# Fourteen row tiles in seven block products, outputs accumulated on PSUM banks that ScalarE copies, token sums in the residual's buffer, and a new order in each group

## The chip, the cores and the metric

The kernel runs on one core of a Trainium2 chip. The metric is the device time of one execution in microseconds (us); the time of the kernel before is the median of three runs, and one further execution was profiled. The engines are TensorE (PE in the profile, PEld for its weight loads), VectorE (DVE), ScalarE (ACT), GpSimd (POOL) and SyncE (SP). Here SP and POOL mainly issue DMAs.

## The reference

One encoder layer on 256 tokens of width 2048, in float32. Most of its work is matrix products:

```python
def _swiglu(u, w_gate, w_up, w_down):
    return (jax.nn.silu(u @ w_gate) * (u @ w_up)) @ w_down
...
        f = _swiglu(_rmsnorm(h, ffn1_pre_g[i]), ffn1_w_gate[i], ffn1_w_up[i], ffn1_w_down[i])
        h = h + 0.5 * _rmsnorm(f, ffn1_post_g[i])
        m = _mixer(_rmsnorm(h, mix_pre_g[i]), w_qkv[i], na_rpb[i], out_g[i], w_o[i])
        h = h + _rmsnorm(m, mix_post_g[i])
        f = _swiglu(_rmsnorm(h, ffn2_pre_g[i]), ffn2_w_gate[i], ffn2_w_up[i], ffn2_w_down[i])
        h = h + 0.5 * _rmsnorm(f, ffn2_post_g[i])
        g = jax.nn.sigmoid(_rmsnorm(h, ple_pre_g[i]) @ w_ple_gate[i])
        h = h + _rmsnorm(g * (p[i] @ w_ple_proj[i]), ple_post_g[i])
```

The hidden width of both feed-forward blocks (FFN1, FFN2) is 5632. The mixer is attention with 16 heads; the last part is a small gated product (PLE).

## The kernel before

**Precision.** A float32 operand is split into a high and a low part (`_h`, `_l`; weights `wh`, `wl`), and a product takes three matmuls for each row tile and token tile: high by high (L104), low by high (L105), high by low (L106), all in `mac`. The tokens are the stationary operand (128x128), the weights stream past (128x512). A row tile is 128 of the 2048 input rows, so there are 16; a token tile is 128 of the 256 tokens, so there are two. `split` (L71) makes the two parts of two row tiles of weights at once: a cast on ACT (L77), a subtraction on DVE (L78), in six buffers each that go round in turn.

**Groups.** Each FFN walks over the hidden width in eleven groups (`nb` 0 to 10) of 512 columns. A group has four outputs, gate and up for two token tiles: g0, g1, u0, u1, each one PSUM bank. Then comes SiLU(gate) times up, eight transposes to `hid` (`tr`), and, within the next group, four "down" blocks of 24 matmuls, which bring the hidden columns of the group before to the width of 2048 and are added to `f` by DVE (L436). `fill()` takes the next waiting down block at fixed places of the group.

**Block products.** Groups 1 to 10 don't compute all outputs by the plain product. `ROWS` (L29) pairs six row tiles with six others. With tokens as a 2x2 block matrix (token tile by half of the rows) and weights likewise (half of the rows by gate or up), `pair_product` (L164) uses the Strassen-Winograd form, seven block products for eight. Three of them have plain tokens (u) as stationary operand: a11, a12 and a22. Four have sums of tokens (`sums_h`, `sums_l`): s1 to s4, made once for each FFN by `token_sums` (L300). The weights of the products are sums too: `add_rows` (L193) adds the up weights to gate weights in place by POOL DMAs that accumulate, and `add` does further ones on DVE (L204). The four row tiles that are left ("rest") are multiplied plainly for all four outputs. The outputs are put together from the products: `kept` (L173) copies a product from PSUM to SBUF on ACT (L175), and DVE adds or subtracts (L206).

**Order.** The engines run their instructions in the order of the program, which a scheduler draws up from the order of the code. A buffer's next writer waits for its last reader. The order in a group before is a11, s4, the transposes of the group before, half of the rest for u, a down block, s1, the other half, down, s2, down, s3, a12, a22, down, the rest for g. Weight loads are issued on SP in this order too, each waiting there until its buffer is free.

```python
        ra1, rb2 = blocks(wa, 0, ca), blocks(wb, 1, cb)
        g1 = bank("g1")
        mac(g1, a11, split_rows(ra1), first=True, last=True)
        g0_ = kept("g0_s", g1)
```

**Around the FFNs.** `h`, the residual, stays in SBUF all the time. `load_h` (L369) loads it in FFN1's group 0, where `prenorm_factor` (L376) squares it. `residual` (L384) adds an FFN's result to it at the end.

Of the kernel before, what the change touches and what calls it, by code (L numbers as in the profile page):

```python
# [15 lines left out]
P = 128  # L16
D = 2048
# [11 lines left out]
ROWS = (0, 1, 2, 3, 8, 9), (4, 5, 6, 7, 10, 11)  # L29
# [5 lines left out]
def encoder_layer(ctx: ExitStack, tc: tile.TileContext, a: dict, out: bass.AP):  # L35
# [35 lines left out]
    def split(raw):  # L71

        n, m = raw.shape[1:]
        wh = wpool.tile([P, 2, NB], F32R, name="wh", bufs=6)[:, :, :m]
        wl = wpool.tile([P, 2, NB], F32R, name="wl", bufs=6)[:, :, :m]
        splits[:] = [
            nc.scalar.copy(wh[:, :n], raw),  # L77
            nc.vector.tensor_tensor(wl[:, :n], raw, wh[:, :n].bitcast(F32), op=ALU.subtract),  # L78
        ]
        return [(wh[:, i], wl[:, i]) for i in range(n)]  # L80
# [83 lines left out]
    def pair_product(lhs, sums, wa, ca, wb, cb, fill, rest_first):  # L164

        rows1, rows2 = ([lhs[k] for k in ks] for ks in ROWS)
        a11, a12, a22 = of_tile(rows1, 0), of_tile(rows2, 0), of_tile(rows2, 1)
        s1, s2, s3, s4 = sums
# [4 lines left out]
        def kept(name, x):  # L173
            t = ffn_pool[0].tile([P, NB], F32, name=name, tag="part", bufs=3)
            nc.scalar.copy(t, x)  # L175
            return t

        def spans(j, step):
            for k0, k1 in ((0, KB), (KB, RQ)):
                for k in range(k0, k1, step):  # L180
                    yield k, min(k + step, k1)
# [5 lines left out]
        def blocks(w, j, c):  # L187
            raw = ffn_pool[0].tile([P, RQ, NB], F32, name="raw_b", bufs=3)
            for k0, k1 in spans(j, KB):
# [3 lines left out]
        def add_rows(raw, w, j, c):  # L193
            for k0, k1 in spans(j, 2):
                nc.gpsimd.dma_start(raw[:, k0:k1], weight_rows(w, j, c, k0, k1), accum_op=ALU.add)  # L195

        def split_rows(raw):
            return sum((split(raw[:, k : min(k + 2, RQ)]) for k in range(0, RQ, 2)), [])

        def add(out_, x, y, op=ALU.add):  # L200
            n = x.shape[1] if len(x.shape) > 2 else 0
            for k in range(0, n, 2):
                j = slice(k, min(k + 2, n))
                nc.vector.tensor_tensor(out_[:, j], x[:, j], y[:, j], op=op)  # L204
            if not n:
                nc.vector.tensor_tensor(out_, x, y, op=op)  # L206

        nk = len(lhs)
        k_rest = [(k, (nk - 2 * RQ) // 2) for k in range(2 * RQ, nk, (nk - 2 * RQ) // 2)]

        def rest(w, k, n, c, accs_, last=False):
            parts = load_parts(w, k * P, n, c)
            for t, acc, lead in accs_:
                mac(acc, of_tile(lhs[k : k + n], t), parts, first=lead, last=last)

        def rest_b(i, last):
            rest(wb, *k_rest[i], cb, [(1, u1, i == 0), (0, u0, i == 0 and rest_first)], last=last)

        u0 = u1 = None
        if rest_first:  # L220
            u0, u1 = bank("u0"), bank("u1")
            rest_b(0, False)
            run_later()
        ra1, rb2 = blocks(wa, 0, ca), blocks(wb, 1, cb)
        g1 = bank("g1")
        mac(g1, a11, split_rows(ra1), first=True, last=True)
        g0_ = kept("g0_s", g1)
        add_rows(ra1, wb, 0, cb)
        u0 = u0 or bank("u0")
        mac(u0, s4, split_rows(rb2), first=not rest_first)  # L230
# [7 lines left out]
        u1_ = kept("u1_s", g0)
        add(ra1, ra1, rb2)
        add_rows(rb2, wb, 0, cb)  # L240
        if not rest_first:
            rest_b(1, True)
        fill()
        mac(g1, s2, split_rows(ra1), last=True)
        u0_ = kept("u0_s", g1)
        add(u0_, u0_, u1_, ALU.subtract)
        ra2 = blocks(wa, 1, ca)
        fill()
        mac(g1, s3, split_rows(rb2), last=True)
        add(u0_, u0, u0_, ALU.subtract)  # L250
        add(u1_, u1_, g1, ALU.subtract)
        add(u1_, u1, u1_)
        mac(g0, a12, split_rows(ra2), first=True)
        add(ra1, ra1, ra2)
        mac(g1, a22, split_rows(ra1))
        fill()
        for k, n in k_rest:
            rest(wa, k, n, ca, [(0, g0, False), (1, g1, False)], last=k + n == nk)
        assert len(k_rest) == 2
        add(g0_, g0, g0_)  # L260
        return (g0_, g1), (u0_, u1_)
# [38 lines left out]
    def token_sums(*parts):  # L300
# [3 lines left out]
        hi, lo = (  # L304
            sums_pool[0].tile([P, 2, 2, n_all, P], F32R, name=f"sums_{x}", tag=f"sums_{x}", bufs=1) for x in "hl"
        )
# [28 lines left out]
    h = resid.tile([P, NT, D], F32, name="h")  # L335
# [13 lines left out]
    def load_x(k):  # L349
# [7 lines left out]
        else:  # L357
            xb = ffn_pool[0].tile([P, 2, S], F32, name="xb", tag="gs", bufs=2)
# [25 lines left out]
    def residual(fg, ssf, scale, blocks, rs, g, sums=None, y_pool=None):  # L384
# [4 lines left out]
        r, y0 = [], []  # L389
        for b0 in range(0, D // NB, 2):  # L390
# [469 lines left out]
```

## Time and profile before

| | |
|---|---|
| time, median of three runs | 1928.42 us (1928.11 to 1928.62) |
| the profiled execution | 1928.43 us, of which its span from first to last instruction is 1926.7 us |
| mean granted clock of TensorE | 0.998 |
| FFN1's groups 1 to 10 and its end, 56.15 to 702.2 us | PE busy 645.43 of 646.05 us |
| attention and its output, 702.2 to 1109.1 us | PE busy 404.13 of 406.90 us |
| FFN2 up to its last groups, 1109.1 to 1742 us | PE busy 632.52 of 632.90 us |
| FFN2's end and PLE, 1742 to 1926.7 us | PE busy 171.26 of 184.70 us |

Rows of a timeline give start, duration, engine, line, operation, output<-inputs and shapes, and in brackets the engine's idle time before it and what ended that. Rows of groups give a count, busy time and mean duration in ns of one, then the idle time before them. A matmul's recorded duration overlaps the next one's; starts tell the pitch.

### The profile page before, as it was taken

The page shows a single profiled execution, that of the slowest core. Times are in us where ns is not written, and L with a number is a line of the kernel's source. Part 1 is how long each engine was busy: PE and PEld are TensorE (multiplying, and loading weights), DVE is VectorE, ACT ScalarE, POOL GpSimd, SP SyncE. Part 2 cuts the span into 40 slices and gives each one's busy share as a digit, 9 for nine tenths or more (in the row PEclk, how much of TensorE's full clock was granted, in tenths as well). Part 3 has the DMA queues.
Part 4 walks back from the last instruction along what each step waited for, and adds up shares of the span by engine and source line. Part 5 has one row for each costly group of instructions (what it writes and reads, how often), then busy time and mean ns, then how long its engine had stood idle before and what let it go on. Part 6 is the DMA issues. An engine that isn't in the chain of part 4 may idle for free.

```text
span 1926.7 us, 23362 instructions
## 1 busy us (share of the span) xinstructions
PE 1902.8 (99%) x8600; PEld 1562.8 (81%) x8600; DVE 1554.7 (81%) x1740; ACT 1128.8 (59%) x1364; POOL 172.4 (9%) x151
## 2 busy tenths in 40 slices
PE   8999999999999999999999999999999999999997
PEld 6888888888888878888888888888888888888786
DVE  7888898889898986666565588888988898889864
ACT  7666565666566554554545466665656655665653
POOL 0111101100110000000000010110011011100100
PEclk9999999999999999999999999999999999999999
DMA  9897778877887647454455568887778777875463
GB/s 350 241 251 232 232 203 228 240 229 223 214 246 234 170 157 247 143 175 155 151 179 182 186 210 238 224 239 233 210 210 248 225 228 212 245 224 162 160 226 114
DMA packets 207363, 408.41 MB, mean 212 GB/s; under 512 B 8849, under 2 KB 11921, under 8 KB 206737
## 3 DMA queue, kind: packets, MB, share of 16 engines
q1 hardware_dynamic: 174608, 344.00, 51.4%
q0 software_dynamic: 32640, 62.92, 18.8%
q8 instruction: 67, 1.10, 0.2%
q14 instruction: 48, 0.39, 0.1%
HBM read 404.79 MB, written 2.10 MB: 211 GB/s over the span
## 4 chain that ended last, share of the span: by engine, by line
PE 95%; DVE 2%; ACT 1%; issue 1%; DMA 1%; POOL 0%; SPq 0%; DVEq 0%; POOLq 0%; ACTq 0%
PE pair_g L105 10%; PE pair_g L104 10%; PE pair_g L106 10%; PE down L105 8%; PE down L104 8%; PE down L106 8%; PE pair_u L104 3%; PE pair_u L105 3%; PE pair_u L106 3%; PE v L106 2%; PE v L105 2%; PE v L104 2%; PE mo L106 1%; PE mo L104 1%; PE mo L105 1%; PE tr L290 1%
## 5 line engine op out<-in xcount | busy, mean ns | idle before, releaser
L77 ACT CAST wh<-raw 128x1024 fp32r<-128x1024 f32 (+1 forms) x453 | 471.7, 1051 | 384.2 <-PE down L105 114.2
L78 DVE TENSOR_TENSOR wl<-raw,wh 128x1024 fp32r<-128x1024 f32 (+1 forms) x453 | 541.6, 1220 | 151.4 <-ACT wh L77 142.9
L77 ACT CAST wh<-raw_b 128x1024 fp32r<-128x1024 f32 x420 | 440.8, 1050 | 280.9 <-PE pair_g L105 126.1
L78 DVE TENSOR_TENSOR wl<-raw_b,wh 128x1024 fp32r<-128x1024 f32 x420 | 507.8, 1222 | 107.4 <-ACT wh L77 97.8
L105 PE MATMUL down<-wh,hid_l 128*128 128x512 f32 x640 | 252.4, 394 | 0.0
L104 PE MATMUL down<-wh,hid_h 128*128 128x512 f32 x640 | 251.3, 393 | 0.0
L106 PE MATMUL down<-wl,hid_h 128*128 128x512 f32 x640 | 249.3, 389 | 0.0
L195 POOL DMA_DIRECT2D raw_b<-in_ffn_w_up x120 | 146.2, 1232 | 1054.7 <-DVE wl L78 727.5
L104 PE MATMUL pair_g<-wh,u_h 128*128 128x512 f32 x520 | 202.5, 389 | 0.0
L106 PE MATMUL pair_g<-wl,u_h 128*128 128x512 f32 x520 | 202.3, 389 | 0.0
L105 PE MATMUL pair_g<-wh,u_l 128*128 128x512 f32 x520 | 202.3, 389 | 0.0
L204 DVE TENSOR_TENSOR raw_b<-raw_b 128x1024 f32<-128x1024 f32 x120 | 144.6, 1221 | 0.1
L104 PEld LDWEIGHTS down<-wh,hid_h 128*128 128x128 f32 x640 | 120.2, 188 | 27.9
L106 PEld LDWEIGHTS down<-wl,hid_h 128*128 128x128 f32 x640 | 120.2, 188 | 27.1
L105 PE MATMUL pair_g<-wh,sums_l 128*128 128x512 f32 x360 | 142.0, 394 | 0.0
L104 PE MATMUL pair_g<-wh,sums_h 128*128 128x512 f32 x360 | 141.7, 394 | 0.0
L106 PE MATMUL pair_g<-wl,sums_h 128*128 128x512 f32 x360 | 140.9, 391 | 0.0
L105 PEld LDWEIGHTS down<-wh,hid_l 128*128 128x128 f32 x640 | 120.4, 188 | 24.5
L436 DVE TENSOR_TENSOR f<-f,down 128x512 f32<-128x512 f32 x160 | 109.1, 682 | 15.8 <-PE down L106 15.7
L104 PEld LDWEIGHTS pair_g<-wh,u_h 128*128 128x128 f32 x520 | 97.6, 188 | 20.4
L106 PEld LDWEIGHTS pair_g<-wl,u_h 128*128 128x128 f32 x520 | 97.6, 188 | 20.3
L105 PEld LDWEIGHTS pair_g<-wh,u_l 128*128 128x128 f32 x520 | 97.6, 188 | 20.2
(218 smaller groups left out, 2947.9 us busy)
## 6 DMA issues: line engine op xcount, KB each, us to landing
raw<-in_ffn_w_down SPq DMA_DIRECT2D x88, 1024.0 KB, 6.7
raw_b<-in_ffn_w_up POOLq DMA_DIRECT2D x120, 512.0 KB, 9.2
raw<-in_w_qkv SPq DMA_DIRECT2D x48, 1024.0 KB, 5.0
raw_b<-in_ffn_w_gate SPq DMA_DIRECT2D x40, 1024.0 KB, 6.0
raw<-in_ffn_w_gate SPq DMA_DIRECT2D x41, 512.0 KB, 6.5
raw<-in_ffn_w_up SPq DMA_DIRECT2D x40, 512.0 KB, 6.8
raw_b<-in_ffn_w_gate SPq DMA_DIRECT2D x40, 512.0 KB, 9.0
raw_b<-in_ffn_w_up SPq DMA_DIRECT2D x20, 1024.0 KB, 5.1
```

The lines of the kernel that those rows point to most:

```text
L77: nc.scalar.copy(wh[:, :n], raw),
L78: nc.vector.tensor_tensor(wl[:, :n], raw, wh[:, :n].bitcast(F32), op=ALU.subtract),
L104: nc.tensor.matmul(acc, xh, wh, start=lead, stop=False, skip_group_check=True)
L105: nc.tensor.matmul(acc, xl, wh, start=False, stop=False, skip_group_check=True)
L106: nc.tensor.matmul(acc, xh, wl, start=False, stop=tail, skip_group_check=True)
L195: nc.gpsimd.dma_start(raw[:, k0:k1], weight_rows(w, j, c, k0, k1), accum_op=ALU.add)
L204: nc.vector.tensor_tensor(out_[:, j], x[:, j], y[:, j], op=op)
L290: nc.tensor.transpose(tr[:, k], x[:, k * P : (k + 1) * P], ident)
L436: nc.vector.tensor_tensor(f_t, f_t, acc, op=ALU.add)
```

## The change

Seven row tiles pair with seven others (`ROWS`), so that fourteen of the sixteen take the block products and two are left as rest. The first pair group of an FFN (`nb` 1, `apart`) keeps six pairs, and takes the two odd row tiles plainly.

In the other groups an output's terms are accumulated in its bank instead of in SBUF. a11 goes to g0, ACT copies that bank to g1's (L240 of the new program), and a12 goes on top of g0. s1 goes to u0, ACT copies it to u1's bank (L249), and s4 goes on top of u0; s2, s3 and a22 go on top of g1, with a copy to SBUF in between (L206). Three of five DVE combines fall away. The new order is a11, transposes, a12, down, s1, down, rest for u, s4, s2, down, s3, a22, rest for g, down. The split buffers go from six to seven.

On PE, where a11 ends (FFN1; the other groups are alike), the rows stood so before, with s4 on `pair_u` in front of the transposes and a rest product behind them (waits in brackets):

```order
L105 MATMUL pair_u_1531<-wh,sums_l 128x512
L106 MATMUL pair_u_1531<-wl,sums_h 128x512
L290 MATMUL tr<-ident,u_s 128x128 [waits DVE_49,PE_49]
L290 MATMUL tr<-ident,u_s 128x128 x3
L290 MATMUL tr<-ident,u_s 128x128 [waits DVE_49,PE_49]
L290 MATMUL tr<-ident,u_s 128x128 x3
L104 MATMUL pair_u_1576<-wh,u_h 128x512 [waits Activation_49]
L105 MATMUL pair_u_1576<-wh,u_l 128x512
```

Now a11 and a12 stand on either side of the transposes, and both write the bank of g0, `pair_g_1520`:

```order
L104 MATMUL pair_g_1520<-wh,u_h 128x512 [waits Activation_49]
L105 MATMUL pair_g_1520<-wh,u_l 128x512
L106 MATMUL pair_g_1520<-wl,u_h 128x512 [waits DVE_49]
L308 MATMUL tr<-ident,u_s 128x128 [waits PE_49]
L308 MATMUL tr<-ident,u_s 128x128 x3
L308 MATMUL tr<-ident,u_s 128x128 [waits DVE_49,PE_49]
L308 MATMUL tr<-ident,u_s 128x128 x3
L104 MATMUL pair_g_1520<-wh,u_h 128x512 [waits Activation_49]
```

The last row's wait on ACT holds the copy of that bank too. On ACT, the copy of a11 stood behind three splits before (of rest and down weights), and wrote SBUF:

```order
L428 ACTIVATE gs<-pair_g_3955,r 128x512
L77 CAST wh<-raw 128x1024 x3
L175 COPY g_s<-pair_g_4447 128x512
L77 CAST wh<-raw_b 128x1024 x3
L296 CAST hid_h<-tr 128x4x128 x2
```

Now, in the same place, it stands behind a12's splits (from `raw_b`) and the two of the next down block (from `raw`), and writes the bank of g1:

```order
L77 CAST wh<-raw_b 128x1024 x2
L77 CAST wh<-raw_b 128x512
L77 CAST wh<-raw 128x1024 x2
L240 COPY pair_g_2027<-pair_g_2026 128x512
L314 CAST hid_h<-tr 128x4x128 x2
L77 CAST wh<-raw_b 128x1024 x3
```

Later in the group, on PE, s3 was followed by a12 in a bank of its own (`pair_g_1633`):

```order
L104 MATMUL pair_g_1495<-wh,sums_h 128x512
L105 MATMUL pair_g_1495<-wh,sums_l 128x512
L106 MATMUL pair_g_1495<-wl,sums_h 128x512
L104 MATMUL pair_g_1633<-wh,u_h 128x512
L105 MATMUL pair_g_1633<-wh,u_l 128x512
L106 MATMUL pair_g_1633<-wl,u_h 128x512 [waits DVE_49]
```

Now four matmuls of the rest on g0 (`pair_g_1520`) stand between s3 and a22, which share the bank of g1 (`pair_g_1521`); a22's first waits for ACT, whose copy of s3's result (u1_s, L206) reads that bank:

```order
L104 MATMUL pair_g_1521<-wh,sums_h 128x512
L105 MATMUL pair_g_1521<-wh,sums_l 128x512
L106 MATMUL pair_g_1521<-wl,sums_h 128x512 [waits DVE_49]
L104 MATMUL pair_g_1520<-wh,u_h 128x512 [waits Activation_49]
L105 MATMUL pair_g_1520<-wh,u_l 128x512
L106 MATMUL pair_g_1520<-wl,u_h 128x512 [waits DVE_49]
L104 MATMUL pair_g_1520<-wh,u_h 128x512
L104 MATMUL pair_g_1521<-wh,u_h 128x512 [waits Activation_49]
```

ACT has one split of down weights in front of that copy, too.

To make room, `sums_h` lies in the residual's buffer. So `h` isn't held during an FFN: x is read once into a weight buffer for its squares, and `load_stream` loads `h` again in the last group, in FFN1 from x and in FFN2 from a copy in DRAM (`h_kept`) that POOL DMAs write at FFN2's start. `gs` moves to a work buffer, the transposed rows kept for the sums take eight buffers instead of six, and the empty fills of the last group but one go.

```diff
-ROWS = (0, 1, 2, 3, 8, 9), (4, 5, 6, 7, 10, 11)
+ROWS = (0, 1, 2, 3, 8, 9, 10), (4, 5, 6, 7, 11, 12, 13)
...
-        wh = wpool.tile([P, 2, NB], F32R, name="wh", bufs=6)[:, :, :m]
-        wl = wpool.tile([P, 2, NB], F32R, name="wl", bufs=6)[:, :, :m]
+        wh = wpool.tile([P, 2, NB], F32R, name="wh", bufs=7)[:, :, :m]
+        wl = wpool.tile([P, 2, NB], F32R, name="wl", bufs=7)[:, :, :m]
...
+        def copied(name, x):
             t = ffn_pool[0].tile([P, NB], F32, name=name, tag="part", bufs=3)
             nc.scalar.copy(t, x)
             return t
...
+        def rest(w, c, accs_, ks=(2 * RQ, 2 * RQ + 1), first=False):
+            raw = wpool.tile([P, 4, NB], F32, name="raw", bufs=3)
+            rows_ = w[:, c : c + NB].rearrange("(k p) n -> p k n", p=P)
+            raw_loads.append(nc.sync.dma_start(raw[:, :2], rows_[:, ks[0] : ks[1] + 1 : ks[1] - ks[0]]))
+            parts = split(raw[:, :2])
+            for t, acc in accs_:
+                mac(acc, of_tile([lhs[k] for k in ks], t), parts, first=first)
...
+        else:
+            ra1 = blocks(wa, 0, ca)
+            g0, g1 = bank("g0"), bank("g1")
+            mac(g0, a11, split_rows(ra1), first=True)
+            nc.scalar.copy(g1, g0)
+            add_rows(ra1, wb, 0, cb)
+            run_later()
+            ra2 = blocks(wa, 1, ca)
+            mac(g0, a12, split_rows(ra2))
+            fill()
+            rb2 = blocks(wb, 1, cb)
             u0, u1 = bank("u0"), bank("u1")
+            mac(u0, s1, split_rows(ra1), first=True)
+            nc.scalar.copy(u1, u0)
+            add(ra1, rb2)
+            fill()
+            rest(wb, cb, [(1, u1), (0, u0)])
+            mac(u0, s4, split_rows(rb2))
+            add_rows(rb2, wb, 0, cb)
+        mac(g1, s2, split_rows(ra1))
+        add(ra1, ra2)
+        u0_ = copied("u0_s", g1)
...
+        combine(u0_, u0, u0_, ALU.subtract)
         fill()
+        mac(g1, s3, split_rows(rb2))
...
+            u1_ = copied("u1_s", g1)
+            combine(u1_, u1, u1_, ALU.subtract)
+        mac(g1, a22, split_rows(ra1))
...
+        rest(wa, ca, [(0, g0), (1, g1)])
...
         fill()
+        return (g0, g1), (u0_, u1_)
...
+        hi = resid.tile([P, 2, 2, n_all, P], F32R, name="sums_h", tag="h")
+        lo = sums_pool[0].tile([P, 2, 2, n_all, P], F32R, name="sums_l", tag="sums_l", bufs=1)
...
+    def load_stream(src):
+        h = stream[0] = resid.tile([P, NT, D], F32, name="h", tag="h")
+        for t in range(NT):
+            nc.sync.dma_start(h[:, t], src(t))
...
+                if sums is not None and b0:
+                    nc.gpsimd.dma_start(h_kept[:, t], h[:, t])
...
+                    if nb == nbs - 1:
+                        load_stream(src)
...
-                if nb == nbs - 2:
-                    waiting[1:1], waiting[3:3] = [None], [None]
```

More of the change, by code (lines that the diff above doesn't have):

```diff
@@ L162, in run_later, with pair_product, spans @@
         later.clear()
[L164 to L168, printed above, removed]
+    def pair_product(lhs, sums, wa, ca, wb, cb, fill, apart):
         def bank(name):
             return ps_acc.tile([P, NB], F32, name=f"pair_{name}", tag="acc")
[L173 to L179, printed above, removed]
+        rq = RQ - apart
+        rows1, rows2 = ([lhs[k] for k in ks[:rq]] for ks in ROWS)
+        a11, a12, a22 = of_tile(rows1, 0), of_tile(rows2, 0), of_tile(rows2, 1)
+        s1, s2, s3, s4 = (x[:rq] for x in sums)
+        def spans(step):
+            for k0, k1 in ((0, KB), (KB, rq)):
                 for k in range(k0, k1, step):
@@ L193, in add_rows @@
         def add_rows(raw, w, j, c):
-            for k0, k1 in spans(j, 2):
+            for k0, k1 in spans(2):
                 nc.gpsimd.dma_start(raw[:, k0:k1], weight_rows(w, j, c, k0, k1), accum_op=ALU.add)
         def split_rows(raw):
[L198 to L206, printed above, removed]
@@ L238, in pair_product @@
[L238 to L242, printed above, removed]
-        fill()
[L244 to L261, printed above, removed]
+            return sum((split(raw[:, k : min(k + 2, rq)]) for k in range(0, rq, 2)), [])
+        def add(x, y):
+            for k in range(0, rq, 2):
+                j = slice(k, min(k + 2, rq))
+                nc.vector.tensor_tensor(x[:, j], x[:, j], y[:, j], op=ALU.add)
@@ new lines, in pair_product @@
+        odd = tuple(ks[RQ - 1] for ks in ROWS)
+        if apart:
+            g0, g1, u0, u1 = (bank(x) for x in ("g0", "g1", "u0", "u1"))
+            rest(wb, cb, [(1, u1), (0, u0)], first=True)
+            run_later()
+            ra1, rb2 = blocks(wa, 0, ca), blocks(wb, 1, cb)
+            mac(g1, a11, split_rows(ra1), first=True)
+            p1 = copied("p1", g1)
+            add_rows(ra1, wb, 0, cb)
+            mac(u0, s4, split_rows(rb2))
+            rest(wb, cb, [(1, u1), (0, u0)], odd)
+            fill()
+            mac(g0, s1, split_rows(ra1), first=True)
+            p5 = copied("p5", g0)
+            add(ra1, rb2)
[7 more added lines that the diff above has]
+            nc.scalar.copy(g1, g0)
+            add_rows(ra1, wb, 0, cb)
+            run_later()
+            ra2 = blocks(wa, 1, ca)
+            mac(g0, a12, split_rows(ra2))
+            fill()
+            rb2 = blocks(wb, 1, cb)
+            u0, u1 = bank("u0"), bank("u1")
+            mac(u0, s1, split_rows(ra1), first=True)
+            nc.scalar.copy(u1, u0)
+            add(ra1, rb2)
+            fill()
+            rest(wb, cb, [(1, u1), (0, u0)])
+            mac(u0, s4, split_rows(rb2))
+            add_rows(rb2, wb, 0, cb)
@@ L263, in accs @@
+        mac(g1, a22, split_rows(ra1))
+        if apart:
+            rest(wa, ca, [(0, g0), (1, g1)], odd)
+        rest(wa, ca, [(0, g0), (1, g1)])
+        if apart:
+            combine(p1, g0, p1, ALU.add)
+            g0 = p1
+        fill()
+        return (g0, g1), (u0_, u1_)
     def accs(name):
@@ L401, in residual @@
                         h[:, t, cols], *blocks[b], t, g[:, b * KB : (b + 1) * KB],
[L402 removed]
+                        **(dict(pool=y_pool, tag="y0", bufs=8) if y_pool is not None else {}),
                     )
[L404 to L405 removed]
+                    y0.append(y)
+                if sums is not None and b0:
+                    nc.gpsimd.dma_start(h_kept[:, t], h[:, t])
                 yield
+        later.append(
+            lambda: rs.extend(prenorm_factor(h[:, t].rearrange("p (b n) -> p b n", n=NB)) for t in range(NT))
+        )
         if sums is not None:
@@ L415, in residual, with swiglu @@
             )
-        later.append(lambda: rs.extend(prenorm_factor(t) for t in range(NT)))
     def square_sums():
         return [small.tile([P, D // NB], F32, name="ssf") for _ in range(NT)]
-    def swiglu(pool, f, ssf, res, blocks, rs, sums, w_gate, w_up, w_down, g_post):
+    def swiglu(pool, f, ssf, res, blocks, rs, sums, w_gate, w_up, w_down, g_post, src):
         lhs = rows(blocks)
```

87 lines of the change are left out of this document (41 added, 46 removed).

## The prediction

> **What bounds the kernel now.** I read the page first, to learn which engine sets the end, and then the stage in which the change lies.
>
> ```profile
> span 1926.7 us, 23362 instructions
> ...
> PE 1902.8 (99%) x8600; PEld 1562.8 (81%) x8600; DVE 1554.7 (81%) x1740; ACT 1128.8 (59%) x1364; POOL 172.4 (9%) x151
> ...
> PE 95%; DVE 2%; ACT 1%; issue 1%; DMA 1%; POOL 0%; SPq 0%; DVEq 0%; POOLq 0%; ACTq 0%
> ```
>
> TensorE (PE) is busy 99% of the span and holds 95% of the chain that ended last; it is idle for 1926.7 - 1902.8 = 24 us in all. Next come two rows of the windows view, each one whole group of 512 columns, from the end of one group's last down block to the end of the next one's, in FFN1 and in FFN2. The columns are length, busy time and count of PE, weight loads, DVE, ACT and POOL, then the granted clock, the DMA share and GB/s.
>
> ```profile
> 172.93:235.40 62.47, 62.47 (x280) 51.53 (x278) 55.84 (x57) 38.03 (x41) 7.30 (x6) 1.00 0.80 227
> 1276.80:1339.75 62.95, 62.95 (x279) 51.53 (x278) 55.85 (x57) 38.04 (x41) 7.29 (x6) 1.00 0.79 225
> ```
>
> Inside a group PE has no gap at all, at full granted clock, with DVE at 89% beside it. So a matmul that is taken away is worth its whole pitch, and anything PE has to wait for is a plain loss. The pitch is read from starts, since the recorded 0.39 us of one matmul overlaps the next. Timeline of PE, FFN1 and then FFN2 (start, duration, engine, line, output<-inputs):
>
> ```profile
> 184.73 0.39 PE L105 MATMUL pair_u<-wh,sums_l 128*128 128x512 f32 x1
> ...
> 186.57 1.04 PE L290 MATMUL tr<-ident,u_s 128*128 128x128 f32 x8
> 187.37 0.48 PE L104 MATMUL pair_u<-wh,u_h 128*128 128x512 f32 x1
> ...
> 195.68 0.39 PE L104 MATMUL pair_g<-wh,sums_h 128*128 128x512 f32 x1
> ...
> 199.80 0.39 PE L104 MATMUL pair_u<-wh,u_h 128*128 128x512 f32 x1
> ...
> 202.52 0.39 PE L104 MATMUL down<-wh,hid_h 128*128 128x512 f32 x1
> ```
>
> ```profile
> 1299.65 0.39 PE L104 MATMUL pair_g<-wh,sums_h 128*128 128x512 f32 x1
> ...
> 1303.85 0.40 PE L104 MATMUL pair_u<-wh,u_h 128*128 128x512 f32 x1
> ```
>
> Three prices follow. Twelve matmuls on the plain tokens (u) take 202.52 - 199.80 = 2.72, or 0.2267 each. Eighteen on the token sums take 199.80 - 195.68 = 4.12 in FFN1, 0.2289 each, and 1303.85 - 1299.65 = 4.20 in FFN2, 0.2333 each. Eight transposes hold PE for 187.37 - 186.57 = 0.80.
>
> **Matmuls removed.** A group had 7 products of 6 rows and 4 rest rows for 4 outputs, 42 + 16 = 58; it has 49 + 8 = 57, three matmuls to each. Three products stand on u and four on sums, so the u matmuls fall from 54 + 48 = 102 to 63 + 24 = 87 and the sums matmuls rise from 72 to 84. This holds for nine groups in each FFN; the first pair group keeps 58. At the old pitches a group gains 15 x 0.2267 - 12 x 0.2289 = 0.65 in FFN1 and 3.40 - 2.80 = 0.60 in FFN2, in all 9 x 1.25 = **11.3 us**.
>
> The sums may also run faster. They do the same work as u at a longer pitch, and only their place in memory differs: in the built program the u tiles begin at multiples of 4096 bytes, the sums at none, and otherwise in each FFN. Now sums_h, which two of three matmuls read, begins at 4096. If those run at 0.2267 and sums_l at the old pitch, 84 of them cost 12.70 + 6.41 = 19.10 in FFN1 and 12.70 + 6.53 = 19.23 in FFN2, against 16.48 and 16.80 for the old 72; the gain is 0.78 and 0.97 a group, 15.7 us. That place is the reason is a guess; I take the middle, **13.5 us**, and keep both ends.
>
> **Two waits added in each group.** The first product of a pair now stays in its PSUM bank, where the next one goes on, and ScalarE (ACT) copies it to a second bank. PE may not add to the bank until the copy has read it. ACT's rows (a timeline, then one line of the groups by form) and the weight load's price:
>
> ```profile
> 182.47 1.06 ACT L77 CAST wh<-raw 128x1024 fp32r<-128x1024 f32 x1
> 183.44 0.57 ACT L175 COPY g_s<-pair_g 128x512 f32<-128x512 f32 x1
> ...
> 185.16 1.05 ACT L77 CAST wh<-raw_b 128x1024 fp32r<-128x1024 f32 x1 [0.21 <-PE pair_u L105]
> ```
>
> ```profile
> L175 ACT COPY u_s<-pair_g 128x512 f32<-128x512 f32 x2 | 1.2, 578 | 0.0
> ```
>
> ```profile
> L104 PEld LDWEIGHTS down<-wh,hid_h 128*128 128x128 f32 x640 | 120.2, 188 | 27.9
> ```
>
> A split (cast) starts 0.04 after the last read of its buffer (184.73 + 0.39 = 185.12, then 185.16), and the next operation follows 0.97 later (182.47 to 183.44). At a12, time 0 being a11's start: 21 matmuls take 4.76, the transposes end at 5.56, and a12 is due. ACT has two splits of the next down block in front of the copy. With seven wh buffers in turn, the second waits for a11's third pair, whose last read is matmul 17: 16 x 0.2267 + 0.39 + 0.04 = 4.06. The copy starts at 5.03 and ends at 5.61; released 0.04 later, a12 comes 0.09 late, or 0.28 if its weight load is held as well. Queued behind the waiting matmul are only PE's own.
>
> At a22, from s3's start: the same split stands before u1_s's copy, 16 x 0.2289 + 0.43 = 4.09, the copy runs from 5.06 to 5.64, and the release is at 5.68. PE has 21 matmuls, 4.80, and four of the rest's, to 5.70. So a22 loses nothing, or 0.17. The bounds are 0.09 and 0.45 a group. I take 0.40, near the upper end, because this trace shows load and matmul starting together after a wait:
>
> ```profile
> 679.76 1.24 PEld L104 LDWEIGHTS down<-wh,hid 128*128 128x128 f32 x6 [0.80 <-ACT hid L296]
> 679.76 1.44 PE L104 MATMUL down<-wh,hid 128*128 128x512 f32 x5 [0.56 <-ACT hid L296]
> ```
>
> 18 x 0.40 = **7.2 us**. The other two copies have cover: u1's has a whole down block behind it (24 matmuls, about 5.5), and u0_s's has one too.
>
> No row shows a copy from PSUM to PSUM. The nearest is the 0.578 above, to SBUF; the 1.05 of a cast of twice the width bounds it above, and a copy with no wait left bounds it below. At 1.05 both waits grow by 0.47, to 1.39 a group, 25 us. I take 0.578, the same size from the same memory.
>
> The Trainium skill (ScalarE: Activation LUTs, "What ACT_TABLE_LOAD costs") gives an activation with immediate operands 186 ns and 0.833 ns an element, 613 ns here; this trace's 578 is shorter, and decides. By 613 ns the two copies would cost 0.07 a group more, 1.3 us in all. Its remark that ScalarE reaches PSUM sooner than SBUF ("Step-by-step: what each stage is for") would shorten them; no run shows it yet.
>
> **Beside PE.** DVE's prices in one FFN1 group:
>
> ```profile
> L78 DVE TENSOR_TENSOR wl<-raw_b,wh 128x1024 fp32r<-128x1024 f32 x21 | 25.4, 1222 | 5.0 <-ACT wh L77 4.5
> ...
> L204 DVE TENSOR_TENSOR raw_b<-raw_b 128x1024 f32<-128x1024 f32 x6 | 7.2, 1220 | 0.0
> ...
> L206 DVE TENSOR_TENSOR u_s<-pair_u,u_s 128x512 f32<-128x512 f32 x2 | 1.4, 688 | 0.0
> ```
>
> Two splits of two rows go (-2.44), seven of one row come (at the 0.69 of the last row, +4.8), two one-row adds come (+1.4), three combines go (-2.1). DVE rises by 1.7, from 55.84 to 57.5 of some 61.8 us, 93%. Following the new order against these times, each split is ready 2 us or more before PE needs it, but for the rest's at s3's end, which comes out level; so I cost this at nothing.
>
> The transfers, from the view of DMA issues (the last column is us to landing):
>
> ```profile
> raw_b<-in_ffn_w_up POOLq DMA_DIRECT2D x120, 512.0 KB, 9.2
> ...
> h<-in_x SPq DMA_DIRECT2D x2, 1024.0 KB, 9.7
> ```
>
> POOL's adding DMAs go from six to eight for 14 instead of 12 row blocks, and a group's weights grow from 54 to 55 blocks: the DMA share goes from 0.80 to about 0.82. Those for s1 are issued once a11's splits are done, by the order before a11 starts; s1 follows 4.76 + 0.80 + 4.76 + 5.5 = 15.8 us after a11's start, against 9.2 to landing. That hides them.
>
> The single events (h stored by two DMAs in FFN2 and reloaded by two in each FFN, x read once more beside the first weights, its squares earlier, no empty fills) fall where PE has a down block or more in hand. The reload starts after the last s3; a22, the rest and the last down blocks pass before its first use, 20 us or more against 9.7. The post gains queue behind it on SP and have the least to spare, about a microsecond if each load takes that long. I put all this at nothing, give or take 2 us.
>
> **The sum.** The profiled execution took 1928.43 us (1.7 outside its span), and the median of the runs is 1928.42. 1928.4 - 13.5 + 7.2 = **1922.1 us**.
>
> **The rivals.** First, no waits: the copy ends inside the cover. Then 1928.4 less 11.3 to 15.7 gives 1912.7 to 1917.1, say 1915. For it: the bounds begin at 0.09. Against it: load and matmul begin together above.
>
> Second, slower: the copies come late. ACT takes its instructions in order, and each copy stands behind a split that starts only 0.7 us before the product ends. A copy at the price of a 1.05 cast makes 1928.4 - 13.5 + 25 = 1939.9. It decides from 13.5 / 18 = 0.75 us a group on. Against it is the 0.578.
>
> Third, DVE becomes a bound of its own at 93%: if the rest's split, level above, comes one 0.69 operation late in each group, 1922.1 + 12.4 = 1934.5. Against it are the 5.0 us that DVE spent waiting before splits in a group.
>
> Fourth, the clock. The longest wait of PE behind the start, and two windows, one with the wait of 0.56 us at 679.76 and one just after this long one:
>
> ```profile
> 705.44 0.50 PE L97 MATMUL q<-wh,u_h 128*128 128x512 f32 x1 [2.20 <-ACT u_h L296]
> ```
>
> ```profile
> 679.20:682.60 3.40, 2.78 (x11) 1.99 (x12) 2.83 (x4) 1.00 (x3) 0.00 (x0) 1.00 1.04 393
> ...
> 707.00:710.40 3.40, 2.99 (x8) 2.15 (x8) 2.95 (x5) 1.63 (x5) 1.46 (x1) 0.53 0.43 106
> ```
>
> A wait of half a microsecond left the clock at 1.00; the one of 2.20 was followed by 0.53 for 3.4 us. If each group lost half of such a window, 18 x 1.7 = 31 us, the end would be 1953. The Trainium skill (TensorE: Matmul & The Clock Gate, "A second HAM failure mode: psum-queue depth-cycling") speaks against the change: small idles between groups of matmuls on cycling banks let the clock swing. The first window speaks against it here.
>
> Fifth, the edges take back 5 us: 1927.
>
> **How the numbers follow.** Chances: forecast 0.43, no waits 0.22, late copies 0.15, DVE 0.08, clock 0.02, edges 0.10. A change within 0.2%, 3.9 us, is about what a measurement of this kernel can't tell from none, so faster means below 1924.6. The forecast, with its own spread of 1919 to 1927, gives 0.31 to faster and 0.12 to the same; no waits gives 0.22 to faster; late copies 0.12 slower and 0.03 the same; DVE 0.04 the same and 0.04 slower; the clock 0.02 slower; the edges 0.03 faster, 0.05 same and 0.02 slower. Faster 0.56, the same 0.24, slower 0.20. The range goes from 1912.7, the low bound of the first rival, to 1934, beyond which lie most of the late copies, the clock and some of DVE, about 0.2 in all.
>
> **What would show it.** A group of 61.8 to 62.2 us in FFN1; PE idle 0.1 to 0.3 before a12 and up to 0.2 before a22, released by ACT's copies; a copy of 0.58; sums matmuls at 389 ns recorded if place is the reason; DVE near 57.5 a group. A copy near 1 us, a clock under 1.00 inside groups, or a new wait for DVE, a DMA or the reloaded h would make the prediction wrong.

## The result and the profile after

The changed kernel takes **1917.71 us** (median of six runs, 1915.72 to 1919.31), the one before 1928.16 (six runs, 1927.63 to 1928.62). The ratio is 0.9945, with a 95% interval of 0.9932 to 0.9957: 10.5 us faster, where 6.3 were forecast. The profiled execution took 1919.31 us, 1.6 above that median and 9.1 below the profiled execution of before. First from the page: the span, the engines, and the chain that ended last.

```profile
span 1917.5 us, 23547 instructions
...
PE 1895.1 (99%) x8546; PEld 1553.7 (81%) x8546; DVE 1584.0 (83%) x1825; ACT 1172.9 (61%) x1476; POOL 217.5 (11%) x189
...
PE 91%; issue 5%; DVE 1%; ACT 1%; DMA 1%; POOL 0%; SPq 0%; POOLq 0%; DVEq 0%; ACTq 0%
```

TensorE still carries the end (what its share of the chain lost went to issue, in which it waits for nothing that the profile shows, and to no other engine); its busy time fell by 7.7 us and its idle time from 24 to 22.4. The windows view gives one whole group of FFN1 and one of FFN2 (columns as in the prediction):

```profile
178.56:240.86 62.30, 62.30 (x277) 50.93 (x275) 57.35 (x61) 40.46 (x47) 9.18 (x8) 1.00 0.83 234
1340.39:1402.62 62.23, 62.23 (x276) 50.91 (x275) 57.32 (x61) 40.34 (x47) 9.16 (x8) 1.00 0.84 235
```

A group became 0.17 us shorter in FFN1 (62.47 before) and 0.72 in FFN2 (62.95), so the eighteen groups give 9 x 0.89 = 8.0 of the 9.1 us; the other 1.1 lie outside them. FFN1's 62.30 lies just above the 61.8 to 62.2 that the prediction named as its sign. DVE (57.35) and the DMA share (0.83) came out nearly as worked out (57.5 and 0.82), and the clock is 1.00.

Now the first added wait, a12 behind the copy of a11's bank. The timeline of that place in an FFN1 group:

```profile
365.46 0.39 PE L104 MATMUL pair_g<-wh,u_h 128*128 128x512 f32 x1
...
369.51 1.05 ACT L77 CAST wh<-raw 128x1024 fp32r<-128x1024 f32 x1 [0.31 <-PE pair_g L105]
...
370.23 1.04 PE L308 MATMUL tr<-ident,u_s 128*128 128x128 f32 x8
370.47 0.57 ACT L240 COPY pair_g<-pair_g 128x512 f32<-128x512 f32 x1
...
371.10 0.19 PEld L104 LDWEIGHTS pair_g<-wh,u_h 128*128 128x128 f32 x1
371.10 0.50 PE L104 MATMUL pair_g<-wh,u_h 128*128 128x512 f32 x1
```

The split of the next down block holds ACT until 370.47, the copy ends at 371.04, and a12's load and matmul both start 0.06 later: 371.10 - 365.46 = 5.64 after a11's start, where the prediction had the release at 5.65 and the transposes done at 5.56. So the start is 0.07 late. Load and matmul do begin together, but behind transposes that was so before as well: in the prediction's rows of before the first u matmul behind them, at 187.37, is recorded with 0.48 too. Most of what a12's product takes beyond 21 x 0.2267 is therefore not new. The second wait, a22 behind the copy of s3's result:

```profile
413.94 1.06 ACT L77 CAST wh<-raw 128x1024 fp32r<-128x1024 f32 x1 [0.34 <-PE pair_g L105]
...
414.90 0.58 ACT L206 COPY u_s<-pair_g 128x512 f32<-128x512 f32 x1
...
415.36 0.67 PE L104 MATMUL pair_g<-wh,u_h 128*128 128x512 f32 x2
...
415.53 0.19 PEld L104 LDWEIGHTS pair_g<-wh,u_h 128*128 128x128 f32 x1 [0.21 <-ACT u_s L206]
```

The load of a22's first weights waits 0.21 for the copy, and the matmul (the second of the x2, the first being the rest's last) is held back with it. From the rest's first matmul to the end of a22 the 33 matmuls take 7.59 to 7.60 in nearly every group, against 33 x 0.2267 = 7.48: 0.11 a group.

The copy that no trace of before showed, from the groups by form of that FFN1 window:

```profile
L206 ACT COPY u_s<-pair_g 128x512 f32<-128x512 f32 x2 | 1.2, 580 | 0.0
...
L249 ACT COPY pair_u<-pair_u 128x512 f32<-128x512 f32 x1 | 0.6, 586 | 0.0
L240 ACT COPY pair_g<-pair_g 128x512 f32<-128x512 f32 x1 | 0.6, 575 | 0.0
```

From PSUM to PSUM it takes 575 and 586 ns, to SBUF 580. The Trainium skill's remark (ScalarE: Activation LUTs, "Step-by-step: what each stage is for") that ScalarE reaches PSUM sooner than SBUF is not seen in these rows.

Last, the pitch on the token sums, from starts: the beginnings of s4, s2, a down block and s3 in FFN1, then of s2 and the down block in FFN2.

```profile
207.69 0.39 PE L104 MATMUL pair_u<-wh,sums_h 128*128 128x512 f32 x1
...
212.55 0.39 PE L104 MATMUL pair_g<-wh,sums_h 128*128 128x512 f32 x1
...
217.41 0.39 PE L104 MATMUL down<-wh,hid_h 128*128 128x512 f32 x1
...
222.90 0.39 PE L104 MATMUL pair_g<-wh,sums_h 128*128 128x512 f32 x1
```

```profile
1374.34 0.40 PE L104 MATMUL pair_g<-wh,sums_h 128*128 128x512 f32 x1
...
1379.19 0.39 PE L104 MATMUL down<-wh,hid_h 128*128 128x512 f32 x1
```

Twenty-one take 4.86 in FFN1, 0.2314 each, longer than the 0.2289 of before, and 4.85 in FFN2, 0.2310, shorter than 0.2333. Neither is the 0.2267 of u. The down block is off that pitch too: 5.49 for 24, or 0.2288.

Counted with these pitches, the 87 u and 84 sums matmuls of a group take 39.16 us in FFN1 against 39.60 before (102 and 72), a gain of 0.44, and in FFN2 39.12 against 39.92, a gain of 0.80. In FFN2 something else went as well. Before, the down block between s2 and s3 ran slower than the other three, in every group of FFN2:

```profile
1316.30 0.40 PE L104 MATMUL down<-wh,hid_h 128*128 128x512 f32 x1
...
1321.90 0.40 PE L104 MATMUL pair_g<-wh,sums_h 128*128 128x512 f32 x1
```

It took 5.60, or 0.2333 a matmul, with no wait inside, where the others on the same hidden rows took 5.49 to 5.51. Why isn't shown. After the change it takes 5.49, so 0.11 more was gained there, 0.91 in all. Since the groups shrank by 0.17 and 0.72, the waits and the rest took back 0.27 and 0.19. Read directly, the transposes' place took 0.07 more than before, a12's product 0.04 more than the first product behind transposes did before, and the rest with a22 0.11, together 0.22.

### The profile page after: what moved, and what is told of

Its sections match the earlier page's. It is cut to its first block, busy times and chain, and to the rows that moved or that the text cites. A ratio compares the mean times of both kernels' runs of the same rounds, so it can differ in the third digit from the quotient of the medians.

```text
span 1917.5 us, 23547 instructions
## 1 busy us (share of the span) xinstructions
PE 1895.1 (99%) x8546; PEld 1553.7 (81%) x8546; DVE 1584.0 (83%) x1825; ACT 1172.9 (61%) x1476; POOL 217.5 (11%) x189
## 4 chain that ended last, share of the span: by engine, by line
PE 91%; issue 5%; DVE 1%; ACT 1%; DMA 1%; POOL 0%; SPq 0%; POOLq 0%; DVEq 0%; ACTq 0%
PE pair_g L104 10%; PE pair_g L105 9%; PE pair_g L106 9%; PE down L104 8%; PE down L105 8%; PE down L106 8%; PE pair_u L105 4%; PE pair_u L104 4%; PE pair_u L106 4%; PE v L106 2%; PE v L104 2%; PE v L105 2%; PE tr L308 1%; PE q L104 1%; PE q L106 1%
## 5 line engine op out<-in xcount | busy, mean ns | idle before, releaser
L77 ACT CAST wh<-raw_b 128x1024 fp32r<-128x1024 f32 (+1 forms) x546 | 514.2, 950 | 296.2 <-PE down L105 158.2
L78 DVE TENSOR_TENSOR wl<-raw_b,wh 128x1024 fp32r<-128x1024 f32 (+1 forms) x546 | 582.3, 1097 | 75.9 <-ACT wh L77 69.0
L77 ACT CAST wh<-raw 128x1024 fp32r<-128x1024 f32 (+1 forms) x417 | 435.2, 1051 | 317.0 <-PE down L105 61.1
L78 DVE TENSOR_TENSOR wl<-raw,wh 128x1024 fp32r<-128x1024 f32 (+1 forms) x417 | 500.6, 1219 | 149.0 <-ACT wh L77 136.5
L191 POOL DMA_DIRECT2D raw_b<-in_ffn_w_up x156 | 180.3, 1197 | 1036.1 <-DVE wl L78 965.7
L105 PE MATMUL pair_g<-wh,u_l 128*128 128x512 f32 x502 | 195.6, 390 | 0.0
L199 DVE TENSOR_TENSOR raw_b<-raw_b 128x1024 f32<-128x1024 f32 (+1 forms) x156 | 164.4, 1096 | 0.1
L105 PE MATMUL pair_g<-wh,sums_l 128*128 128x512 f32 x288 | 113.8, 395 | 0.0
L104 PE MATMUL pair_g<-wh,sums_h 128*128 128x512 f32 x288 | 113.7, 395 | 0.0
L106 PE MATMUL pair_g<-wl,sums_h 128*128 128x512 f32 x288 | 112.3, 390 | 0.0
```

Source lines behind the costliest of these rows:

```text
L104: nc.tensor.matmul(acc, xh, wh, start=lead, stop=False, skip_group_check=True)
L105: nc.tensor.matmul(acc, xl, wh, start=False, stop=False, skip_group_check=True)
L106: nc.tensor.matmul(acc, xh, wl, start=False, stop=tail, skip_group_check=True)
L199: nc.vector.tensor_tensor(x[:, j], x[:, j], y[:, j], op=ALU.add)
```

## The experiments

Three questions stayed: whether place in memory makes the pitch, what the two waits are worth and whether they can be removed, and how near DVE is to being the bound. In the table "group" is one whole group of FFN1 and of FFN2, by windows, or (a range, or one figure) from the first transposes of one group to those of the next, in both FFNs. Each ratio is to runs of the kernel before taken beside that kernel (medians 1927.5 to 1928.2); kernels with one run have no interval.

| kernel | us, median (runs) | ratio to before, 95% | group, FFN1 / FFN2 |
|---|---|---|---|
| before | 1928.16 (6) | | 62.47 / 62.95 |
| after | 1917.71 (6) | 0.9945 [0.9932, 0.9957] | 62.30 / 62.23 |
| e4_six: after, six pairs everywhere | 1922.49 (1) | | 62.76 / 62.63 |
| e3_twice: after, both copies made twice | 1932.58 (1) | | 63.07 |
| e1_pads: after, two pads | 1905.46 (4) | 0.9881 [0.9867, 0.9896] | 61.66 / 61.67 |
| e5_before_pads: before, the same pads | 1915.09 (4) | 0.9932 [0.9919, 0.9945] | 62.09 / 62.09 |
| e6_offsets: after, other pads | 1910.49 (1) | | 61.64 / 62.01 |
| e2_order: after, two splits behind the copies | 1930.76 (10) | 1.0016 [1.0006, 1.0026] | 62.7 to 63.4 |
| e7_first_copy: after, the first of these | 1935.55 (1) | | 62.6 to 64.1 |
| e9_early_combine: after, one combine earlier | 1918.89 (1) | | 62.2 to 62.6 |
| e8_best: pads, first reordering, a22 covered | 1936.86 (6) | 1.0048 [1.0034, 1.0061] | 62.5 to 65.6 |
| e10_best_queue: e8_best, two DVE places moved | 1902.76 (4) | 0.9867 [0.985, 0.9883] | 61.59 / 61.57 |

**Six pairs everywhere (e4_six).** All groups take the path of the first one: six pairs, a11 and s1 copied to SBUF instead of to a second bank, and a12 between s3 and a22, so that PE waits for neither copy; the new places in memory and all the rest of the change stay.

```diff
-                    gate, up = pair_product(lhs, sums, w_gate, c0, w_up, c0, fill, nb == 1)
+                    gate, up = pair_product(lhs, sums, w_gate, c0, w_up, c0, fill, True)
```

> The changed kernel with every pair group as its first one: six pairs, the two odd row tiles plainly, products kept in SBUF; all else (h reloaded, sums in its buffer, seven split buffers) stays. Theory count: three matmuls come back in each of 18 groups, 0.63 us at the changed kernel's pitches, and the waits of about 0.2 go, so 0.4 a group and 8 us in all: 1925 to 1926. Rival (the gain lies in the other parts): 1917 to 1919.

```profile
178.29:241.05 62.76, 62.76 (x279) 51.53 (x278) 55.47 (x57) 37.90 (x40) 7.35 (x6) 1.00 0.81 223
1343.90:1406.53 62.63, 62.63 (x279) 51.52 (x278) 55.48 (x57) 37.90 (x40) 7.33 (x6) 1.00 0.81 225
```

A group is 0.46 and 0.40 longer than in the changed kernel, 7.7 us over the eighteen; the whole time is 4.8 above the median after, since the part behind FFN2 was 3.3 us shorter in this run. So the seventh pair, with its accumulation on the banks and its waits paid, earns nearly 8 us in the groups.

**The copies made twice (e3_twice).** Each of the two copies that PE waits for is made once more; the values do not change.

```diff
             nc.scalar.copy(g1, g0)
+            nc.scalar.copy(g1, g0)
...
             u1_ = copied("u1_s", g1)
+            nc.scalar.copy(u1_, g1)
```

> The changed kernel with both of these copies made twice, the result being the same. Theory wait: each release comes 0.47 to 0.57 us later, so a12 starts 6.1 to 6.2 us after a11 and a22 as much later, about 1.0 a group, and the time grows by 18 to about 1936. Rival (the copies are covered): less than 2 us.

Timeline of e3_twice at a12; a11 started at 431.64:

```profile
437.67 0.58 ACT L241 COPY pair_g<-pair_g 128x512 f32<-128x512 f32 x1
437.82 0.19 PEld L104 LDWEIGHTS down<-wh,hid_h 128*128 128x128 f32 x1 [0.59 <-ACT hid_h L316]
...
438.30 0.19 PEld L104 LDWEIGHTS pair_g<-wh,u_h 128*128 128x128 f32 x1 [0.30 <-ACT pair_g L241]
438.31 0.50 PE L104 MATMUL pair_g<-wh,u_h 128*128 128x512 f32 x1
```

a12 starts 6.67 after a11 instead of 5.64, and instead of the 6.1 to 6.2 expected, since the scheduler set a cast of hid_h between the two copies. It also put one matmul of the next down block into the gap, which in its turn waits for ACT. So a12's place lost 1.03 less that matmul's 0.23, or 0.8. At a22 next to nothing was lost, for four matmuls of a down block were placed ahead of it there. The time is 14.9 us above the median after, 0.8 a group, and above that of before (1927.49 beside this run). A longer copy does come out as time on PE, as the second rival has it; how much depends on what the scheduler can put in front.

**Place in memory (e1_pads, e5_before_pads, e6_offsets).** Two unused tiles move what is allocated behind them: 64 bytes push the work buffers up, and 480 push FFN2's sums down.

```diff
+    nc.gpsimd.memset(small.tile([P, 16], F32, name="pad", bufs=1), 0.0)
...
+        nc.gpsimd.memset(f_pool.tile([P, 120], F32, name="pad2"), 0.0)
```

With them sums_l and the hidden rows (hid_h, hid_l) begin at multiples of 512 bytes in the built program; the pads do the same for both sums and the hidden rows in the kernel before. Without them these tiles begin 448 bytes past such a multiple (FFN1's sums, all hidden rows) or 480 past (FFN2's sums); only the changed kernel's sums_h begins at 4096.

> Two unused pads (64 bytes per partition ahead of the FFN pools, 480 above the sums in FFN2) let sums_l and both hid tiles begin at multiples of 512 bytes, as u and sums_h do; nothing else changes. Theory place (a stationary tile that begins off a multiple of 512 makes its matmuls slower): 21 sums matmuls take 4.76 us instead of the 4.86 of the changed kernel, 24 down matmuls 5.44 instead of 5.49, so a group loses 4 x 0.10 + 4 x 0.05 = 0.6 us and the time falls from 1917.7 by 11 us to about 1907. Rival (the distance between the high and the low tile, or what else lies near them, sets the pitch): 4.86 and 5.49 stay, time 1917.7 within 2.

Timeline of e1_pads, the same four beginnings as above, and its window:

```profile
452.74 0.39 PE L105 MATMUL pair_u<-wh,sums_h 128*128 128x512 f32 x1
...
457.50 0.39 PE L105 MATMUL pair_g<-wh,sums_h 128*128 128x512 f32 x1
...
462.26 0.39 PE L105 MATMUL down<-wh,hid_h 128*128 128x512 f32 x1
...
467.70 0.39 PE L105 MATMUL pair_g<-wh,sums_h 128*128 128x512 f32 x1
```

```profile
423.84:485.50 61.66, 61.66 (x277) 50.86 (x276) 57.16 (x61) 40.58 (x47) 9.19 (x8) 1.00 0.83 233
```

Twenty-one sums matmuls now take 4.76 and a down block 5.44: 0.2267 each, u's pitch. Nothing else was touched, and 12.2 us went, 9 x (0.64 + 0.56) = 10.8 of them in the groups. The distance between the high and the low part isn't the reason: hid_h and hid_l were both moved by 64 bytes, and their pitch fell. For the kernel before:

> The kernel before with the same two pads, so that its sums (both parts) and hid begin at multiples of 512 bytes. Theory place: 18 sums matmuls take 4.08 us (4.12 in FFN1 and 4.20 in FFN2 without), 24 down matmuls 5.44 instead of 5.50; a group loses 0.36 in FFN1 and 0.78 in FFN2, in all some 11 us: 1917. The change itself is then worth 1905.5 - 1917 = -11.5 with place taken out. Rival (the pads helped through the new layout only): 1928.

```profile
371.56:433.65 62.09, 62.09 (x279) 51.50 (x278) 55.80 (x57) 38.10 (x41) 7.31 (x6) 1.00 0.81 228
```

13.1 us went there. So at equal place the change is worth 1915.09 - 1905.46 = 9.6 us, of which the groups give 18 x (62.09 - 61.66) = 7.7. That is the prediction's counting without any difference of place: 57 products instead of 58, so three matmuls fewer a group, 3 x 0.2267 = 0.68, less 0.25 for the waits. In these two windows the 0.25 can be read: the transposes' place 0.87 against 0.79, the first product behind them 0.14 over its pitch against 0.09, and the rest with a22 7.60 against 7.48.

e6_offsets has other sizes, 320 and 96 bytes. Now the hidden rows begin 256 bytes past a multiple of 512 in both FFNs, sums_l 256 past in FFN1 and 384 past in FFN2, with sums_h on a multiple of 4096.

```diff
+    nc.gpsimd.memset(small.tile([P, 80], F32, name="pad", bufs=1), 0.0)
...
+        nc.gpsimd.memset(f_pool.tile([P, 24], F32, name="pad2"), 0.0)
```

> The changed kernel with other pads: hid begins 256 bytes past a multiple of 512, sums_l 256 past one in FFN1 and 384 past one in FFN2, sums_h at a multiple. Theory 512: 21 sums matmuls 4.86, 24 down 5.49, as in the changed kernel. Theory 128 or 256 (a smaller step is enough): 4.76 and 5.44 where the offset is a multiple of that step, so a time near 1906 for 128.

```profile
178.24:239.88 61.64, 61.64 (x277) 50.86 (x276) 57.13 (x61) 40.56 (x47) 9.18 (x8) 1.00 0.83 234
1333.36:1395.37 62.01, 62.01 (x276) 51.00 (x275) 57.24 (x61) 40.52 (x47) 9.17 (x8) 1.00 0.83 235
```

FFN1 is as fast as with the first pads, FFN2 is 0.37 slower, its 84 sums matmuls taking 4.85 for 21. So 256 past is as good as 0, and 128 past a multiple of 256 is not: the step is 256 bytes. What was moved in these kernels is the operand of the weight loads, 128x128; the buffers of the moving one, wh or wl, begin on multiples of 4096 throughout.

**Removing the first wait (e2_order, e7_first_copy).** The splits of the next down block are placed behind the copy of a11's bank in ACT's order; in e2_order those of the block behind a22 also go behind s3's copy.

```diff
-            nc.scalar.copy(g1, g0)
+            cp = nc.scalar.copy(g1, g0)
...
-            fill()
+            with tc.issue_after(cp.ins):
+                fill()
...
-        fill()
+            fill()
+        else:
+            with tc.issue_after(last_copy[0].ins):
+                fill()
```

> The changed kernel with the splits of the first and the last down block of a group queued behind the copies g1<-g0 and u1_s on ScalarE, instead of ahead of them. Theory wait (PE waits for the copy, and the copy for the split ahead of it): a12's first matmul starts 5.57 us after a11's instead of 5.64; a22 keeps its 0.1, since one rest matmul less stands in front of it; about 0.07 a group, 1.3 us, 1916.4. Rival (what a group has lost beside its pitches isn't the copies): no start moves, 1917.7.

> The changed kernel with only the first of the two reorderings of e2: the first down block's splits behind the copy g1<-g0. Theory wait: the transposes and the wait behind them take 0.82 instead of 0.87, rest and a22 keep 7.59: 0.9 us less in all, 1916.8. Rival (what made e2 slower was this half: DVE's queue is moved by it): a wait for DVE of 0.5 to 0.9 a group appears, 1928 to 1931.

Both missed by 14 to 19 us, and on the other side. In both, a12 did what was expected: the transposes' 0.87 fell to 0.82. But PE has a new wait, in all eighteen groups of e2_order and in fifteen of e7_first_copy. The waits view of e2_order (total, times, longest), then its PE timeline at the rest's first matmuls:

```profile
PE pair_g L106 <- DVE wl L78: 11.7, 18, 1.3
```

```profile
228.13 0.40 PE L105 MATMUL pair_g<-wh,u_l 128*128 128x512 f32 x1
228.78 0.50 PE L106 MATMUL pair_g<-wl,u_h 128*128 128x512 f32 x1 [0.26 <-DVE wl L78]
```

The third matmul of the rest waits for DVE's split of its weights, the one that the prediction called level. Neither edit touches that split; what changed is DVE's order ahead of it. DVE in the changed kernel, where s3 starts at 222.90:

```profile
207.50 2.36 DVE L199 TENSOR_TENSOR raw_b<-raw_b 128x1024 f32<-128x1024 f32 x2
...
211.51 1.82 DVE L199 TENSOR_TENSOR raw_b<-raw_b 128x1024 f32<-128x1024 f32 x2
...
218.94 0.69 DVE L202 TENSOR_TENSOR u_s<-pair_u,u_s 128x512 f32<-128x512 f32 x1
...
226.74 1.23 DVE L78 TENSOR_TENSOR wl<-raw,wh 128x1024 fp32r<-128x1024 f32 x1 [0.59 <-ACT wh L77]
```

And in e2_order, where s3 starts at 223.03:

```profile
210.62 4.09 DVE L199 TENSOR_TENSOR raw_b<-raw_b 128x1024 f32<-128x1024 f32 x4
...
219.96 0.69 DVE L202 TENSOR_TENSOR u_s<-pair_u,u_s 128x512 f32<-128x512 f32 x1 [0.71 <-ACT u_s L206]
...
227.51 1.22 DVE L78 TENSOR_TENSOR wl<-raw,wh 128x1024 fp32r<-128x1024 f32 x1
```

The scheduler now sets the four row adds in one piece instead of two and two, and the splits behind them come later. ACT's copy u0_s then comes 0.9 us later too (the casts ahead of it start 1.2 later, about as much as DVE's splits do; the profile names a DMA or DVE as what released them). So the combine, which now stands in DVE's order ahead of s3's third split, waits 0.71 for the copy, with all of that behind it. The rest's split starts 4.48 after s3's start instead of 3.84. In the changed kernel it waited 0.59 for its own cast, which was the margin, and it is gone.

**Which of the two it is (e9_early_combine, e8_best, e10_best_queue).** e9_early_combine leaves the adds in two pieces and sets only the combine ahead of s3's later splits.

```diff
-        combine(u0_, u0, u0_, ALU.subtract)
+        done = combine(u0_, u0, u0_, ALU.subtract)
...
+            s3_w = split(rb2[:, :2]) + split(rb2[:, 2:4])
+            with tc.issue_after(done.ins):
+                s3_w += split(rb2[:, 4:6]) + split(rb2[:, 6:7])
```

> The changed kernel with one thing forced: VectorE's combine of u0_s, which waits for ScalarE's copy after s2, stands in its queue ahead of s3's third split instead of behind it, as it happened to stand in e2 and e8 (two additions to f move by one place with it). Theory queue (what made e2, e7 and e8 slower is this place): VectorE waits about 1 us there, the rest's split after s3 comes that much later, PE waits 0.5 to 0.9 a group for it, and the time is 1927 to 1934. Rival (the moved splits of the first down block or the adds of a22's weights did it): 1917 to 1919.

DVE in e9_early_combine, where s3 starts at 223.31:

```profile
219.35 0.69 DVE L202 TENSOR_TENSOR u_s<-pair_u,u_s 128x512 f32<-128x512 f32 x1 [1.06 <-ACT u_s L206]
...
227.15 1.23 DVE L78 TENSOR_TENSOR wl<-raw,wh 128x1024 fp32r<-128x1024 f32 x1
```

The combine waits 1.06 us in this kernel, yet the rest's split starts 3.84 after s3's start, as in the changed kernel, and the time is 1.2 above its median, within the spread of those runs. The copy u0_s starts as early here as in the changed kernel, 4.57 ahead of s3. So the waiting combine alone does not cost it.

e8_best puts together the pads, the first reordering, and a22 behind the rest's first six matmuls on g0 and ahead of the other six, so that the copy of s3's result has cover (parts of the diff shown above are left out).

```diff
-        mac(g1, a22, split_rows(ra1))
...
-        rest(wa, ca, [(0, g0), (1, g1)])
+            a22_w = split_rows(ra1)
+            rest(wa, ca, [(0, g0), (1, g1)], between=lambda: mac(g1, a22, a22_w))
```

> e1 with that first reordering, and with the rest's six matmuls on g0 all ahead of a22 instead of four. Theory wait: a12 0.05 earlier, a22 no longer late (33 matmuls in 7.48 instead of 7.59), 0.16 a group and 2.9 us less than e1's 1905.5: 1902.6. Rival (DVE's thin margin at the rest's split): a wait for DVE between s3 and a22 that gives it back, 1905 or more.

```profile
PE pair_g L107 <- DVE wl L79: 21.9, 18, 2.2
```

Its waits view shows the same new wait in all eighteen groups, 1.2 us in the mean. e10_best_queue keeps the adds in one piece and moves only two DVE instructions out of the way: the combine behind s3's last split, and the second addition to f behind a22's second split.

```diff
-        combine(u0_, u0, u0_, ALU.subtract)
...
+            with tc.issue_after(splits[1].ins):
+                combine(u0_, u0, u0_, ALU.subtract)
...
-                nc.vector.tensor_tensor(f_t, f_t, acc, op=ALU.add)
+                added[:] = [nc.vector.tensor_tensor(f_t, f_t, acc, op=ALU.add)]
```

> e8 with that combine forced behind s3's last split, and the second addition to f behind a22's second split, as in the changed kernel. Theory queue: the wait for VectorE goes; what e8 was to bring comes, 1902.6. Rival (the four adds of a22's weights, which stand in one piece here, or the first reordering itself hold VectorE up): a wait of 0.5 us or more for VectorE stays in each group, 1914 or more.

```profile
178.57:240.16 61.59, 61.59 (x276) 50.93 (x275) 56.67 (x61) 40.13 (x47) 9.18 (x8) 1.00 0.83 234
```

No wait for DVE is left in the eighteen groups, and the time is 1902.76 us, 34 below e8_best with the same arithmetic. It is the fastest version here, 0.9867 [0.985, 0.9883] of the kernel before; of the 2.7 us below e1_pads, the groups explain 18 x 0.08 = 1.4. Adds in one piece do no harm without the waiting combine (e10_best_queue), nor the waiting combine without them (e9_early_combine); the loss was there in each kernel that had both (e2_order, e7_first_copy, e8_best). The late copy by itself does no harm either: in e10_best_queue u0_s starts only 2.82 ahead of s3. Which of the two moves of e10_best_queue was needed wasn't separated.

## Why the prediction was right

The forecast was 1922.1 and the time 1917.71, within the range and on the side that had most of the chance. It lies 4.4 below the forecast, outside the 1919 to 1927 that the prediction gave it as its own spread, and 2.7 above the 1915 of the first rival. The mechanism held; two terms of the sum were mis-sized, in opposite senses, so that part of the error cancelled.

- **What bounds it.** PE, without gaps, at full clock: it held. e4_six prices the removed matmuls with their waits at 7.7 us in the groups, close to the balance of the prediction's two terms, 13.5 - 7.2 = 6.3.
- **Matmuls removed, 13.5 taken (11.3 to 15.7).** By the pitches measured, 9 x (0.44 + 0.80) = 11.2, just under the lower bound, and 1.0 from FFN2's slow down block, which the sum did not hold. That the total of 12.2 lies inside the bounds is luck: FFN1's 0.44 is below both of its ends (0.65 and 0.78). That place makes the pitch is now shown (e1_pads, e5_before_pads, e6_offsets). The step that failed is the one after it, that with sums_h on 4096 two of three matmuls would take 0.2267 and the third its old pitch: with sums_l off a multiple of 256, FFN1's sums became slower, 0.2314 against 0.2289, and FFN2's only a little faster, 0.2310 against 0.2333. Nor did the prediction see that the down block's hidden rows lay off as well.
- **Two waits, 7.2 taken (0.09 to 0.45 a group).** Measured about 0.27 and 0.19 a group, 4.1 us. The model of ACT's order came out almost to the figure: a12 5.64 after a11 where 5.65 was worked out, the copy 0.575 where 0.578 was taken. The failed step is the choice of 0.40: of the 0.19 added for load and matmul beginning together, most was paid before, behind the same transposes, and a22 lost 0.11.
- **Beside PE, at nothing.** Right for the changed kernel: DVE 57.35 (57.5), no wait for a split inside its groups. But "level" was as near as it looked: in three kernels of the experiments PE waited 11 to 22 us there.
- **Single events, nothing give or take 2.** Outside the groups the profiled execution became 1.1 us shorter: the mixer by 0.9 and the FFNs' first groups by most of the rest, while the part behind FFN2 grew by 1.3. That last part, from PLE's first matmul to the end, varied between 114.0 and 118.6 us from kernel to kernel; its causes weren't separated.
- **The rivals.** No waits: the waits exist, though smaller. Late copies: not here, but twice the copy cost 0.8 a group (e3_twice). DVE as the bound: not here, but true once the order slips (e2_order, e7_first_copy, e8_best). The clock: 1.00 in both windows although PE now waits twice in each group. The Trainium skill's warning of small idles between matmul groups on cycling banks (TensorE: Matmul & The Clock Gate, "A second HAM failure mode: psum-queue depth-cycling") isn't borne out by these waits of about 0.2 us and less.

That the median is 1.6 below the profiled execution, and that the new runs spread over 3.6 us where the old ones spread over 1.0, stays open.

## What to carry to other kernels

Where TensorE has no gaps, read its pitch from starts for each operand, and where one operand's is longer, look at where its tiles begin: here two shifts of less than 512 bytes were worth more than the whole change. A copy in front of PE costs what is left of it behind the instructions ahead in its engine's order, so work out that order before the copy's length. On an engine busy 92% of a stage, an edit that gained 0.05 us a group cost PE a wait of 0.65 by a reordering elsewhere; look for an instruction that waits with urgent ones behind it, and move that.

## What the runs showed of the hardware

- A stationary operand that begins on a multiple of 256 bytes gives a pitch of 0.2267 us for a 128x128 by 128x512 fp32r matmul. Both parts 192 past a multiple: 0.2289; both 224 past: 0.2333; the high part on and the low part 128, 192 or 224 past: 0.2310 to 0.2314. In a product that reads both, one part on and one off can so be slower than both off. Place alone doesn't settle it: in the kernel before, FFN2's down block between s2 and s3 took 0.2333 with both parts 192 past, the others 0.229. The recorded lengths show it as 389 ns on and up to 396 off, the weight loads (188 ns) not at all. Why isn't known from these runs.
- ACT copies 128x512 f32 from PSUM to PSUM in 575 to 586 ns, and to SBUF in 580; a cast of 128x512 from SBUF to SBUF takes 620 in the same window.
- The first matmul behind transposes holds PE some 0.1 us longer than the pitch (12 u matmuls behind them took 190.18 - 187.37 = 2.81 before, 2.72 elsewhere), with or without a wait.
